# Output projection of two row blocks by seven block products instead of eight, in a hybrid attention layer

## The chip, the cores and the metric

The kernel runs on one core of a Trainium2 chip. A core has a matrix engine (TensorE; "PE" in the profile, and "PEld" for its weight loads), VectorE ("DVE"), ScalarE ("ACT"), GpSimd ("POOL") and SyncE ("SP"), which here only starts DMAs. Each engine works through its own queue in order and waits for the others by semaphores. Weights come from DRAM into SBUF by 16 DMA engines; matmuls write to eight banks of PSUM. The metric is the device time of one execution in microseconds, the median of several runs.

## The reference

One decoder layer for 512 tokens and 1024 channels, in float32. What matters here is the end of its first sub-layer:

```
merged = sigmoid(g_a) * (y_fox @ w_fox_proj) + sigmoid(g_b) * (y_sb @ w_sb_proj)
attn_out = merged @ w_o                                # (512, 1024) @ (1024, 1024)
x = layer_norm(ALPHA * x + (1 + gt1) * attn_out, ln1_g, ln1_b)
```

`y_fox` and `y_sb` are the outputs of two attention branches with eight heads each, `g_a` and `g_b` columns of the input projection, and `gt1` a row of 1024 numbers that comes from a modulation vector. Behind it stands a gated MLP with its own layer norm.

## The kernel before

**Numbers.** Every product of two float32 matrices is made of three matmuls: each operand is split into a high part (rounded, by ScalarE, `hi_of`) and a low part (the rest, by VectorE, `lo_of`), and `mm3` adds high by high, high by low and low by high in PSUM. The down projection of the MLP already forms its row blocks by seven block products instead of eight (`blocks`, `product`, `phase`).

**Weights.** All weight tiles go through one list of items, each a source in DRAM and a procedure (`add_item`). `weights(i)` first issues loads on SyncE's queue up to four items ahead, into `raw` tiles of 128x1024 with five buffers (`LOADS`); a load also waits until the item four places before it has been read (`paced`). Then it calls the procedures of up to two items ahead (`AHEAD`). `split_proc` makes `wh` and `wl`, 128x1024, with three buffers each (`WBUFS`). Items of the modulation (`ada_proc`, VectorE at L241) are held back until the next item has been processed. Only SyncE's queue keeps the program's order; the other engines' queues are ordered by a planner at compile time, which also hands out whichever buffer of a tag comes free.

**Heads and filler.** The 16 heads run one after the other (`stage_a` scores, `stage_b` transposes, `stage_c` values), the stick-breaking branch first. Between the stages `fill` takes matmuls from `stream`, a list of generators in a fixed order: projections of later heads (`proj`), branch projections (`bproj`), gates (`add_gate`: 24 matmuls and a sigmoid). After the last head the rest of `stream` runs: five gates and the eight fox projections. `bproj` for the fox branch, multiplied by its gate (L656) and added to the other branch's (`merge`, L766), gives one of eight 128x512 tiles of `merged`, transposed (channels by tokens), as `mh` and `ml`.

**Output projection.** `wo_proc` takes 128 rows of w_o, multiplies them by `gt[0]` (the row 1 + gt1) on VectorE at L662, and splits both halves of 512 columns into `woh`, `wol`. These small tiles come from one pool, `z`, of 58 (`NZ`). `o_mm(i, ks)` makes row block i (128 tokens) for both column halves: eight channel tiles, three matmuls each, L922 to L924. Row blocks 0 and 1 are taken in two turns, five channel tiles and then three (`CUT`); `o_norm` adds x and normalises; block 2 follows, `o_turn` transposes blocks 0 and 1, then block 3. The up projection begins with tokens 0 to 255 of its first three tiles. Before the change GpSimd multiplies in the stick-breaking heads (L561) and issues small DMAs; `gate_rows` makes `gt[0]` with it long before the last heads.

Of the kernel before, what the change touches and what calls it, by code (L numbers as in the profile page):

```python
# [8 lines left out]
F32 = mybir.dt.float32  # L9
F32R = mybir.dt.float32r  # L10
# [6 lines left out]
P = 128  # L17
# [26 lines left out]
SS = 10  # L44
GTILES = (3, 5, 7, 8, 12, 16, 20, 24)
WARM = 5, 3, 1
CUT = 5
FILL = (15, 18, 18), (11, 11, 11)


# [1 line left out]
def layer_kernel(ctx: ExitStack, tc: tile.TileContext, out, xT, x, c8, wa0, wa1, bcol, w1, wct, wv, bf,  # L52
# [6 lines left out]
    t13 = [tc.dram_tile([P, 1024], F32, name=f"t13_{p}") for p in range(FP)]  # L59
    wgt = [tc.dram_tile([P, 512], F32, name=f"wgt_{q}") for q in range(FP)]  # L60
    t24 = tc.dram_tile([P, 1024], F32, name="t24")
    grow = [tc.dram_tile([1, D], F32, name=f"grow{i}") for i in range(2)]
    st1 = ExitStack()
    stg = ctx.enter_context(tc.tile_pool(name="stg", bufs=1))
# [25 lines left out]
    def hi_of(o, i, scale=1.0):  # L90
        S.activation(o, i, AF.Copy, scale=scale)

    def lo_of(o, i, hi):
        state["read"] = V.tensor_tensor(o, i, fl(hi), ALU.subtract)  # L94
        return state["read"]
# [52 lines left out]
    def z(dt, s, shape=(P, 512)):  # L148
        return zp.tile(list(shape), dt, name=nm(s), tag="z", bufs=NZ)
# [5 lines left out]


    reads, held, pins, convs = [], [], {}, []
    items, depth = [], [LOADS - 1]
    def add_item(src, proc, cols=1024):
        items.append([src, proc, cols, None, None])  # L160
        return len(items) - 1

    def weights(i, ahead=AHEAD):
        while state["load"] < min(len(items), i + depth[0]):
            it = items[state["load"]]
            if it[2] == 512:
                late = state.get("late")
                it[3] = late.tile([P, 512], F32, name=nm("rl"), tag="rl", bufs=4) if late else z(F32, "rs")
            else:
                it[3] = stg.tile([P, 1024], F32, name=nm("raw"), tag="raw", bufs=LOADS)  # L170
            c = 0
            for src in it[0] if isinstance(it[0], list) else [it[0]]:
                w = src.shape[-1]
                d = nc.sync.dma_start(it[3][:, c : c + w], src)
# [10 lines left out]
        while state["proc"] < min(len(items), i + 1 + ahead):  # L185
            process()
        return items[i][4]

    def release():
        while held:  # L190
# [4 lines left out]

    def process():
        it = items[state["proc"]]
        if state["proc"] in pins:
# [12 lines left out]
        reads.append(state["read"])  # L211
        release()
# [302 lines left out]
    def proj(n, after):  # L515
        ps = bank()
        h, l = weights(n)
        for k in range(KT):
            c = slice(k * P, (k + 1) * P)
            mm3(ps, h[:, c], l[:, c], uh[k], ul[k], k == 0, k == KT - 1)  # L520
            yield 3
        after(ps)

    def stage_a(br, h):
# [120 lines left out]
            S.activation(sg[(br, j)], ps, AF.Sigmoid)  # L645
        return f

    def bproj(br, j, n, after):
        ps = bank()
        h, l = weights(n)  # L650
        for q in range(4):
            c = slice(((j % 2) * 4 + q) * P, ((j % 2) * 4 + q + 1) * P)
            mm3(ps, h[:, c], l[:, c], yh[(br, q)], yl[(br, q)], q == 0, q == 3)
            yield 3
        m = sg.pop((br, j))
        V.tensor_tensor(m, ps, m, ALU.mult)  # L656
        after(m)

    woh, wol = [], []

    def wo_proc(r):
        V.tensor_tensor(r, r, gt[0], ALU.mult)  # L662
        h = [z(F32R, "woh") for _ in range(2)]
        l = [z(F32R, "wol") for _ in range(2)]
        for e in range(2):
            c = slice(e * 512, (e + 1) * 512)
            hi_of(h[e], r[:, c])
            lo_of(l[e], r[:, c], h[e])
        woh.append(h)
        wol.append(l)  # L670

    def wdc_proc(r):
        h = [z(F32R, "wdh") for _ in range(2)]
# [28 lines left out]
    marks = {}  # L702
    seq = PAIRS

    def add_proj(n, after):
        stream.append((proj, (add_item(wct[TILES.index(n)], split_proc), after)))
        flush_sum(len(stream))

    def flush_sum(n):
# [2 lines left out]

    wpi = {}

    def add_bproj(br, j, after):
        if j % 2 == 0:
            wpi[br] = add_item(wp[br, j // 2], split_proc)
        stream.append((bproj, (br, j, wpi[br], after)))
# [36 lines left out]
    bj = list(range(KT))  # L755
    for p, nb in (6, 3), (7, 5):
        add_pair(p)
        for _ in range(nb):
            j = bj.pop(0)
            add_bproj(1, j, lambda m, j=j: ma.__setitem__(j, m))  # L760

    mh, ml = [], []

    def merge(j):
        def f(m):
            V.tensor_tensor(m, m, ma[j], ALU.add)  # L766
            a, b = z(F32R, "mh"), z(F32R, "ml")
            hi_of(a, m)
            lo_of(b, m, a)
            mh.append(a)  # L770
            ml.append(b)
        return f

    wos = [0]

    def add_wo():
        if wos[0] < KT:
            add_item(wo[wos[0]], wo_proc)
            wos[0] += 1

    for j in range(3):
        add_gate(0, j)
    marks["y0"] = len(stream)
    flush_sum(1 << 30)
    for j in range(KT):
        add_bproj(0, j, merge(j))
        if j < 5:
            add_wo()
        if j + 3 < KT:
            add_gate(0, j + 3)  # L790
    skip[0] = 0
    add_ada(24 - adas[0])
    while wos[0] < KT:
        add_wo()
    last_wo = len(items) - 1

    cur = {"n": 0, "g": None}

# [108 lines left out]
    x1 = []  # L907
    lnr = []

    o_st = {}  # L910

    def o_mm(i, ks):
        tb = slice(i * P, (i + 1) * P)
        if i not in o_st:
            xn = [z(F32, "xn") for _ in range(2)]
            for e in range(2):
                nc.sync.dma_start(xn[e], x[tb, e * 512 : (e + 1) * 512])
            o_st[i] = xn, [bank(), bank()]
        ps2 = o_st[i][1]
        for e in range(2):  # L920
            for k in ks:
                PE.matmul(ps2[e], mh[k][:, tb], woh[k][e], start=k == 0, stop=False)  # L922
                PE.matmul(ps2[e], mh[k][:, tb], wol[k][e], start=False, stop=False)  # L923
                PE.matmul(ps2[e], ml[k][:, tb], woh[k][e], start=False, stop=k == KT - 1)  # L924

    def o_norm(i):
        xn, ps2 = o_st.pop(i)
        st = cons.tile([P, 2, 6], F32, name=nm("st"), tag="st", bufs=2)
        for e in range(2):
            ps = ps2[e]  # L930
            V.scalar_tensor_tensor(xn[e], xn[e], ALPHA, ps, ALU.mult, ALU.add)
            V.bn_stats(st[:, e, :], xn[e])
        mu, rs = ln_stats(st)
        for e in range(2):
            V.tensor_scalar(xn[e], xn[e], mu, rs, ALU.subtract, ALU.mult)
        x1.append(xn)
# [134 lines left out]
            m = mm3(ps[:, ts], h[:, c], l[:, c], u2h[:, k, ts], u2l[:, k, ts], k == 0, k == KT - 1)  # L1071
        return m

    for ks in (range(CUT), range(CUT, KT)):
        for i in range(2):
            o_mm(i, ks)
            if ks[-1] == KT - 1:
                o_norm(i)
    for i in range(2, NB):
        o_mm(i, range(KT))  # L1080
        o_norm(i)
        for t in ((0, 1), (2,))[i - 2]:
            o_turn(t)
# [252 lines left out]
def _pack(inputs):  # L1336
# [30 lines left out]
    wpj = np.stack([a["w_fox_proj"], a["w_sb_proj"]]).reshape(2, 4, P, 4, 2, P)  # L1367
    r["wp"] = c(wpj.transpose(0, 3, 2, 4, 1, 5).reshape(2, 4, P, D))
    r["wo"] = c(a["w_o"].reshape(KT, P, D))
# [33 lines left out]
```

## Time and profile before

| | |
|---|---|
| median of 3 runs | 735.8 us (735.76 to 736.32) |
| the profiled execution | 736.08 us, its span 734.3 us |
| granted TensorE clock, mean | 0.997 |
| busy: TensorE, VectorE, ScalarE, GpSimd | 724.3, 599.7, 390.1, 84.5 us |
| matmuls | 3442 |
| DMA | 131.96 MB, of which 12.85 MB written |

Times in the profile count from the first instruction. The last stage of the last head ends near 284.4 us, the last fox projection near 333.7 us, the output projection of blocks 0 to 2 near 366.3 us. A line such as "L94 DVE TENSOR_TENSOR wl<-raw,wh 128x1024" names the source line, the engine, the operation, what it writes and reads, and its size; then come its count, its total and mean time, and the idle time of the engine just before it with what ended it. In a timeline row the first number is the start and the second the duration. A stretch row ("284.40:333.65") gives its length and, for each engine, the busy time in it with the count of instructions, then the clock, the share of the DMA engines and GB/s.

### The profile page before, as it was taken

Reading aid. Unit: us, or ns where it says so; the run is one execution under the profiler, and the core shown is the slowest. Engines: PE = TensorE matmul, PEld = TensorE weight load, DVE = VectorE, ACT = ScalarE, POOL = GpSimd, SP = SyncE. Lnnn points to the kernel's source line nnn. Section 1 sums busy time; section 2 is a strip of 40 time slices with the busy share of each in tenths; the row PEclk is TensorE's granted clock in tenths of the full one; section 3 lists DMA queues with packets and bytes.
Section 4 is the critical chain, followed back from the end, with each engine's and each line's share of the span. In section 5 each row is a group of like instructions: output and inputs, shape, how many; then the busy total and the mean of one; then the engine's idle time right before and its main releaser. Section 6 shows DMA issues by size and latency. Waiting matters only on the chain.

```text
span 734.3 us, 9843 instructions
## 1 busy us (share of the span) xinstructions
PE 724.3 (99%) x3442; PEld 604.8 (82%) x3442; DVE 599.7 (82%) x1049; ACT 390.1 (53%) x681; POOL 84.5 (12%) x140
## 2 busy tenths in 40 slices
PE   8999999999999999999999999999999999999995
PEld 5888888888888888888889888888888888888885
DVE  7878799778899896883697999977887878679996
ACT  5576466596885755432065644444453544346550
POOL 1026224343010000000000001000011001000010
PEclk9999999999999999999999999999999999999998
DMA  9944534523332242632075687577799767656734
GB/s 351 404 167 147 196 116 160 185 65 119 135 117 79 95 153 77 206 145 86 1 258 134 218 249 230 177 242 229 206 345 248 212 224 212 214 168 219 228 83 92
DMA packets 45203, 131.96 MB, mean 180 GB/s; under 512 B 6137, under 2 KB 6657, under 8 KB 45153
## 3 DMA queue, kind: packets, MB, share of 16 engines
q1 hardware_dynamic: 37888, 112.61, 44.3%
q0 software_dynamic: 4224, 10.30, 7.4%
q10 hardware_dynamic: 3040, 8.42, 3.1%
q8 instruction: 27, 0.44, 0.2%
q14 instruction: 24, 0.19, 0.1%
HBM read 118.39 MB, written 12.85 MB: 179 GB/s over the span
## 4 chain that ended last, share of the span: by engine, by line
PE 98%; DVE 1%; DMA 0%; issue 0%; DVEq 0%
PE ps L152 19%; PE ps L154 19%; PE ps L153 19%; PE ps L361 6%; PE ps L1131 5%; PE ps L1133 5%; PE ps L1132 5%; PE ps L599 3%; PE ps L581 2%; PE ps L507 2%; PE ps L509 2%; PE ps L508 2%; PE ps L924 2%; PE ps L922 2%; PE ps L923 2%; PE ps L533 1%
## 5 line engine op out<-in xcount | busy, mean ns | idle before, releaser
L217 ACT ACTIVATE wh<-raw 128x1024 fp32r<-128x1024 f32 (+1 forms) x105 | 109.2, 1042 | 107.4 <-PE ps L153 35.2
L94 DVE TENSOR_TENSOR wl<-raw,wh 128x1024 fp32r<-128x1024 f32 (+2 forms) x114 | 137.8, 1210 | 34.2 <-ACT wh L217 33.5
L152 PE MATMUL ps<-u2h,wh 128*128 128x512 f32 (+1 forms) x376 | 141.3, 376 | 0.0
L153 PE MATMUL ps<-u2l,wh 128*128 128x512 f32 (+1 forms) x376 | 141.2, 375 | 0.0
L154 PE MATMUL ps<-u2h,wl 128*128 128x512 f32 (+1 forms) x376 | 141.2, 375 | 0.0
L154 PEld LDWEIGHTS ps<-u2h,wl 128*128 128x128 f32 x376 | 70.8, 188 | 12.9
L152 PEld LDWEIGHTS ps<-u2h,wh 128*128 128x128 f32 x376 | 70.8, 188 | 12.7
L153 PEld LDWEIGHTS ps<-u2l,wh 128*128 128x128 f32 x376 | 70.8, 188 | 12.7
L152 PE MATMUL ps<-uh,wh 128*128 128x512 f32 x200 | 79.5, 398 | 0.0
L154 PE MATMUL ps<-uh,wl 128*128 128x512 f32 x200 | 78.3, 391 | 0.0
L153 PE MATMUL ps<-ul,wh 128*128 128x512 f32 x200 | 77.9, 390 | 0.0
L1184 ACT ACTIVATE cv<-ps,cw 128x512 f32<-128x512 f32 x44 | 34.0, 773 | 46.2 <-PE ps L154 36.2
L1185 DVE SCALAR_TENSOR_TENSOR cv<-ps,cw,cv 128x511 f32<-128x511 f32 x44 | 32.8, 745 | 22.6 <-ACT cv L1184 22.5
L154 PEld LDWEIGHTS ps<-uh,wl 128*128 128x128 f32 x200 | 37.5, 188 | 8.6 <-DVE wl L94 0.3
L153 PEld LDWEIGHTS ps<-ul,wh 128*128 128x128 f32 x200 | 37.6, 188 | 7.5
L152 PEld LDWEIGHTS ps<-uh,wh 128*128 128x128 f32 x200 | 37.5, 188 | 7.3
L241 DVE SCALAR_TENSOR_TENSOR raw<-raw,cbc 128x1024 f32<-128x1024 f32 x32 | 39.6, 1238 | 0.0
L561 POOL TENSOR_TENSOR pt<-pt,om 128x127 f32<-128x127 f32 (+3 forms) x32 | 38.5, 1213 | 1.6 <-DVE om L560 1.5
L181 POOL DMA_DIRECT2D raw<-in_wdp x10 | 8.8, 884 | 245.1 <-DMA raw<-in_wdp 208.4
L1186 DVE SCALAR_TENSOR_TENSOR cv<-ps,cw,cv 128x510 f32<-128x510 f32 x44 | 32.7, 743 | 0.4
L1192 ACT ACTIVATE cv<-cv 128x512 f32<-128x512 f32 x22 | 13.9, 631 | 34.1 <-DVE cv L1186 34.1
L560 DVE TENSOR_TENSOR_SCAN om<-om,dg 128x127 f32<-128x127 f32 (+3 forms) x32 | 27.1, 907 | 2.9 <-ACT om L555 2.9
(238 smaller groups left out, 1552.5 us busy)
## 6 DMA issues: line engine op xcount, KB each, us to landing
raw<-in_wup SPq DMA_DIRECT2D x44, 512.0 KB, 4.7
raw<-in_wa SPq DMA_DIRECT2D x32, 512.0 KB, 3.5
raw<-in_wct SPq DMA_DIRECT2D x25, 512.0 KB, 4.5
raw<-in_wdp SPq DMA_DIRECT2D x20, 512.0 KB, 5.6
wa<-in_wa SPq DMA_DIRECT2D x16, 512.0 KB, 8.6
raw<-in_wdp SPq DMA_DIRECT2D x22, 256.0 KB, 4.5
raw<-t SPq DMA_DIRECT2D x22, 256.0 KB, 4.1
raw<-in_wdp POOLq DMA_DIRECT2D x10, 512.0 KB, 7.4
```

What stands on the lines that cost most here:

```text
L94: state["read"] = V.tensor_tensor(o, i, fl(hi), ALU.subtract)
L152: PE.matmul(ps, wh, ah, start=first, stop=False)
L153: PE.matmul(ps, wh, al, start=False, stop=False)
L154: return PE.matmul(ps, wl, ah, start=False, stop=last)
L217: state["hi"] = S.activation(h[:, 0:cols], r[:, 0:cols], AF.Copy)
L241: state["read"] = V.scalar_tensor_tensor(wt[:, c], wt[:, c], 1.0, cbc[:, c] if by is None else by, ALU.mult, ALU.mult, accum_out=o)
L361: PE.matmul(grp[g], w, u, start=j == 0 and n == 0, stop=j == KT - 1 and n == (1 if g == 7 else 2))
L561: G.tensor_tensor(pt[b][:, s : e - 1], pt[b][:, s : e - 1], om[:, s + 1 : e], ALU.mult)
L1131: PE.matmul(ps, ah, bh, start=first, stop=False, skip_group_check=onto)
L1132: PE.matmul(ps, ah, bl, start=False, stop=False, skip_group_check=onto)
L1133: return PE.matmul(ps, al, bh, start=False, stop=last, skip_group_check=onto)
L1184: S.activation(t, ps, AF.Identity, bias=cw[:, n, 3:4], scale=cw[:, n, 2:3])
```

## The change

Write the first two row blocks and the four pairs of 128-row blocks of scaled w_o as 2x2 blocks. Their product takes seven block products a pair: `wo_five` makes five, on five PSUM banks (`ob`: `pa`, `y`, `z2`, `zz`, `w`) that stay taken from its first call on, and two more are added onto `pa` and `w` after `pa` has been copied and `w` subtracted. The column sums of `merged` that they need are made on VectorE and ScalarE by `wo_sums`, right after the second tile of a pair is merged; so fox projections and gates run in the order `JO` (0, 4, 1, 5, ...).

The sums of the weight blocks are made by GpSimd. w_o is packed in pairs and loaded once as eight raw items during the last heads (`add_scale`: pair 0 behind the projections of the seventh pair of heads, pair 1 behind those of the eighth, pairs 2 and 3 behind the second and third gate). `scale_a` and `scale_b` multiply it by `gt[0]` and store it in DRAM (`swo`), form the sums and store them (`two`). Later `swo` is loaded as items for `wo_proc`, which now only splits, and `two` as items for `split_proc`, used by `wo_five`. A list `live` keeps `weights` from processing ahead while all three `wh` buffers are in use. Block 2's first three channel tiles run before the last `wo_five`.

```diff
+JO = (0, 4, 1, 5, 2, 6, 3, 7)
...
+    def scale_a(p):
+        def f(r):
+            G.tensor_tensor(r, r, gt[0], ALU.mult)
+            G.dma_start(swo[p][:, 0:1024], r)
+            return r
+        return f
+
+    def scale_b(p, k):
+        def f(r):
+            a, lo, hi = items[k][4], slice(0, 512), slice(512, 1024)
+            G.tensor_tensor(r[:, lo], r[:, lo], gt[0][:, hi], ALU.mult)
+            G.tensor_tensor(r[:, hi], r[:, hi], gt[0][:, lo], ALU.mult)
+            G.dma_start(swo[p][:, 1024:2048], r)
+            G.tensor_tensor(a[:, lo], a[:, lo], a[:, hi], ALU.add)
+            G.tensor_tensor(a[:, hi], a[:, hi], r[:, lo], ALU.add)
+            G.dma_start(two[p][:, 1024:2048], a)
+            G.tensor_tensor(r[:, lo], r[:, lo], a[:, lo], ALU.add)
+            G.tensor_tensor(r[:, hi], r[:, hi], r[:, lo], ALU.add)
+            G.dma_start(two[p][:, 0:1024], r)
+        return f
...
-        V.tensor_tensor(r, r, gt[0], ALU.mult)
...
+    def wo_sums(p):
+        a, o = mraw.pop(p), mraw.pop(p + 4)
+        s, h, l = z(F32, "os"), z(F32R, "oh"), z(F32R, "ol")
+        c = [slice(q * P, (q + 1) * P) for q in range(4)]
+        V.tensor_tensor(s[:, c[0]], a[:, b1], a[:, b0], ALU.subtract)
+        V.tensor_tensor(s[:, c[1]], o[:, b0], a[:, b0], ALU.subtract)
+        V.tensor_tensor(s[:, c[2]], s[:, c[1]], a[:, b1], ALU.add)
+        V.tensor_tensor(s[:, c[3]], s[:, c[2]], o[:, b1], ALU.subtract)
...
+        hi_of(h[:, n], s[:, n])
+        lo_of(l[:, n], s[:, n], h[:, n])
+        hi_of(s4[0][:, c[p]], s[:, c[3]])
+        lo_of(s4[1][:, c[p]], s[:, c[3]], s4[0][:, c[p]])
...
+    def wo_five(p, ta, tb):
...
+        h, l = weights(ta, 3)
+        pa, y, z2, zz, w = ob
+        todo = [(y, so[p][2], (h[:, lo], l[:, lo])), (z2, (mh[p + 4][:, b0], ml[p + 4][:, b0]), (h[:, hi], l[:, hi])),
+                (pa, (mh[p][:, b1], ml[p][:, b1]), (woh[p][0], wol[p][0]))]
+        for n in (0, 1, 2) if p < 3 else (0, 2, 1):
+            wo_mm(*todo[n], *ends)
+            yield 3
+        used(ta)
+        h, l = weights(tb, 3)
+        for ps, a, c in ((zz, 0, hi), (w, 1, lo)):
+            wo_mm(ps, so[p][a], (h[:, c], l[:, c]), *ends)
+            yield 3
+        used(tb)
...
-    for ks in (range(CUT), range(CUT, KT)):
-        for i in range(2):
-            o_mm(i, ks)
-            if ks[-1] == KT - 1:
-                o_norm(i)
...
+    S.activation(p1, pa, AF.Copy)
+    V.tensor_tensor(u2, p1, y, ALU.subtract)
+    V.tensor_tensor(u3, u2, zz, ALU.add)
+    V.scalar_tensor_tensor(xa[0], xa[0], ALPHA, z2, ALU.mult, ALU.add)
+    V.scalar_tensor_tensor(xa[1], xa[1], ALPHA, u3, ALU.mult, ALU.subtract)
+    V.tensor_tensor(xa[0], xa[0], u3, ALU.add)
+    V.tensor_tensor(xa[1], xa[1], w, ALU.subtract)
+    o_norm(0, xa)
+    V.scalar_tensor_tensor(xb[1], xb[1], ALPHA, u2, ALU.mult, ALU.subtract)
+    o_mm(2, range(3, 4))
+    for k in range(4):
+        wo_mm(pa, (mh[k + 4][:, b1], ml[k + 4][:, b1]), (woh[k + 4][0], wol[k + 4][0]), False, k == 3, True)
+    for k in range(4):
+        wo_mm(w, so[k][3], (woh[k + 4][1], wol[k + 4][1]), False, k == 3, True)
+    V.scalar_tensor_tensor(xb[0], xb[0], ALPHA, pa, ALU.mult, ALU.add)
+    V.tensor_tensor(xb[1], xb[1], w, ALU.subtract)
+    o_norm(1, xb)
```

The order of the late stream, with b for a fox projection, g for a gate, f for `wo_five` and w for the load and split of a scaled half pair: b0 g3 w b1 g4 f0 b2 w g5 b3 g6 f1 w g7 b4 w b5 w b6 w b7 f2 w, block 2's first three tiles, f3 w.

More of the change, by code (lines that the diff above doesn't have):

```diff
@@ new lines, in wo_mm @@
+    def wo_mm(ps, a, b, first, last, onto=False):
+        PE.matmul(ps, a[0], b[0], start=first, stop=False, skip_group_check=onto)
+        PE.matmul(ps, a[0], b[1], start=False, stop=False, skip_group_check=onto)
+        PE.matmul(ps, a[1], b[0], start=False, stop=last, skip_group_check=onto)
+    def wo_five(p, ta, tb):
+        if p == 0:
+            ob.extend(bank() for _ in range(5))
+        lo, hi, ends = slice(0, 512), slice(512, 1024), (p == 0, p == 3)
+        h, l = weights(ta, 3)
[11 more added lines that the diff above has]
+        used(tb)
@@ new lines, in add_five, with add_wo, first_rows0, rest @@
+    def add_five(p):
+        ta, tb = add_ring(two[p][:, 0:1024]), add_ring(two[p][:, 1024:2048])
+        stream.append((wo_five, (p, ta, tb)))
+    def add_wo(p, n):
+        add_item(swo[p][:, n * 1024 : (n + 1) * 1024], wo_proc(p + 4 * n, ((0, 1), (1, 0))[n]))
+    xab = []
+    def first_rows0():
+        xab.append(o_rows(0))
+        yield 0
+    def rest(i, ks):
+        o_mm(i, ks)
+        yield 0
+    for n in range(3):
+        add_gate(0, JO[n])
+        if n:
+            add_scale(n + 1)
@@ L797, in layer_kernel, with o_mm @@
+    def o_mm(i, ks):
+        tb = slice(i * P, (i + 1) * P)
+        if i not in o_st:
+            o_st[i] = [bank(), bank()]
+        for e in range(2):
+            for k in ks:
+                wo_mm(o_st[i][e], (mh[k][:, tb], ml[k][:, tb]), (woh[k][e], wol[k][e]), k == 0, k == KT - 1)
     cur = {"n": 0, "g": None}
@@ L908, in layer_kernel, with o_norm @@
     lnr = []
[L910 to L915, printed above, removed]
+    def o_norm(i, xn=None):
+        st = cons.tile([P, 2, 6], F32, name=nm("st"), tag="st", bufs=2)
+        if xn is None:
+            ps2, xn = o_st.pop(i), o_rows(i)
             for e in range(2):
-                nc.sync.dma_start(xn[e], x[tb, e * 512 : (e + 1) * 512])
-            o_st[i] = xn, [bank(), bank()]
-        ps2 = o_st[i][1]
+                V.scalar_tensor_tensor(xn[e], xn[e], ALPHA, ps2[e], ALU.mult, ALU.add)
         for e in range(2):
[L921 to L931, printed above, removed]
             V.bn_stats(st[:, e, :], xn[e])
```

143 lines of the change are left out of this document (100 added, 43 removed).

## The prediction

> **What bounds the kernel now.** I read the page's busy line first, then the chain that ended last, then TensorE's own waits, and last the busy time of the stretches that the change touches.
>
> ```profile
> span 734.3 us, 9843 instructions
> PE 724.3 (99%) x3442; PEld 604.8 (82%) x3442; DVE 599.7 (82%) x1049; ACT 390.1 (53%) x681; POOL 84.5 (12%) x140
> PE 98%; DVE 1%; DMA 0%; issue 0%; DVEq 0%
> PE ps L230 <- DVE warm L107: 1.2, 1, 1.2
> PE ps L230 <- DVE wa L241: 0.6, 2, 0.3
> PE ps L361 <- DVE uh L329: 0.3, 1, 0.3
> 284.40:333.65 49.25, 49.25 (x219) 40.33 (x218) 40.49 (x57) 22.28 (x34) 0.00 (x0) 1.00 0.44 153
> 333.65:366.30 32.65, 32.65 (x146) 27.04 (x145) 14.39 (x31) 4.18 (x7) 0.00 (x0) 1.00 0.14 48
> 200.00:284.40 84.40, 84.40 (x440) 72.05 (x439) 72.42 (x157) 54.76 (x114) 2.05 (x4) 1.00 0.29 101
> ```
>
> TensorE is 98% of the chain, and the three rows are all of its waits on others: 2.1 us, at the start. The stretch rows give busy time of TensorE, weight loads, VectorE, ScalarE, GpSimd. From 200 to 366 us, where everything in the diff lies, TensorE is busy without a gap, so a matmul removed there comes off the end, unless a new wait takes its place. 284.4 to 333.65 us is the last gates and fox projections, 333.65 to 366.3 the output projection of row blocks 0, 1 and 2. It has 144 matmuls (two blocks' 96, block 2's 48) and the tail of two before it, so one costs 32.65 / 144 = 0.2267 us. (Rows call a matmul 389 ns; that is its pipelined length.)
>
> **The matmuls.** Before, blocks 0 and 1 take 2 x 2 x 8 x 3 = 96. After, `wo_five` runs five products of three, four times: 60; the two late loops, onto `pa` and `w`, 12 each: 84. Block 2 keeps 48, only moved. Twelve go: 12 x 0.2267 = **2.72 us**. That is the whole gain.
>
> **What VectorE and ScalarE get.** Columns below: line, engine, shape, count, then total and mean ns.
>
> ```profile
> L662 DVE TENSOR_TENSOR raw<-raw,gt 128x1024 f32<-128x1024 f32 x8 | 9.8, 1220 | 1.0 <-DMA raw<-in_wo 0.9
> L94 DVE TENSOR_TENSOR wol<-raw,woh 128x512 fp32r<-128x512 f32 x16 | 10.7, 683 | 0.0
> L94 DVE TENSOR_TENSOR wl<-raw,wh 128x1024 fp32r<-128x1024 f32 x7 | 8.5, 1221 | 2.9 <-ACT wh L217 2.9
> L217 ACT ACTIVATE wh<-raw 128x1024 fp32r<-128x1024 f32 (+1 forms) x105 | 109.2, 1042 | 107.4 <-PE ps L153 35.2
> L550 DVE TENSOR_SCALAR pt<-pt,sm 128x128 f32<-128x128 f32 (+3 forms) x32 | 10.2, 383 | 0.3
> L94 DVE TENSOR_TENSOR ptc<-ps,ptc 128x384 fp32r<-128x384 f32 x16 | 8.7, 546 | 0.0
> L91 ACT ACTIVATE ptc<-ps 128x384 fp32r<-128x384 f32 x16 | 7.9, 493 | 0.1
> 333.53 0.39 PE L154 MATMUL ps<-yh,wl 128*128 128x512 f32 x1
> 333.96 0.69 DVE L656 TENSOR_TENSOR sg<-ps,sg 128x512 f32<-128x512 f32 x1 [0.23 <-PE ps L154]
> 335.17 0.68 DVE L766 TENSOR_TENSOR sg<-sg,sg 128x512 f32<-128x512 f32 x1
> ```
>
> The scaling by `gt` leaves VectorE: 9.8 us less, 7.3 of it after 284.4. Added there: eight splits of the sums, 8 x 1.22 = 9.8 (ScalarE 8 x 1.04 = 8.3); four `wo_sums`, each four 128-column operations (at most 0.38), one low half of 384 (0.55) and one of 128 (0.38), about 2.4 each, 9.8 in all; and two `wol` splits more than the window had, 1.4. So 40.5 - 7.3 + 21 = 54 us in a stretch that grows by 60 + 18 matmuls to 49.25 + 17.7 = 67 us: 81%, against 82% now. ScalarE goes to about 33 of 67. Neither becomes the bound on average. Locally: the last fox matmul starts at 333.53, the merged sum ends at 335.85, 2.3 us later. Four sums (1.5), high (0.5) and low half (0.55) bring the first products' operand at about 4.9 us. `wo_five` 0 to 2 stand behind a gate, 24 matmuls or 5.4 us; number 3 behind 15 + 18, 7.5 us. So they are covered, by half a microsecond where VectorE is free at once, and not if a 1.22 us split is in front; an operand late by that costs 0.7 us at one place. I take 0.3 us in all, with 0 and 3 (four places) as bounds.
>
> **The end.** The copy of `pa` must be done before the late loop adds onto `pa`, and `xa[1] - w` before the loop onto `w`; TensorE's queue holds the rest of block 2 behind both. `pa` closes nine matmuls before `wo_five` ends; one ScalarE copy then has that 2.0 us and 6 more matmuls (1.4). After the copy VectorE has six operations of 0.69, ending about 2.5 us after `w` closes, where 18 matmuls (4.1 us) stand. `o_norm(1)` follows the last of the 24: two operations, two statistics and a chain that takes 5 us, beside 24 matmuls, 5.4 us. Covered, thinly; zero, at most 1 us. The transposes and the first up weights then move with the rest.
>
> **GpSimd, DRAM and SyncE's queue.** GpSimd gets 28 operations and 16 stores of 512 KB; SyncE's queue gets 24 loads for w_o where it had 8, and the first eight now stand ahead of weights that TensorE needs sooner. That is 8.4 MB stored and 8.4 MB more loaded over some 150 us, 112 GB/s beside the 101 and 153 of the stretch rows at shares of 0.29 and 0.44: the DMA engines are not filled. Block 0's `x` loads move ahead of `wo_five` 3's; the tiles that they take came free with the last projection's inputs, so they hold up nothing.
>
> ```profile
> L561 POOL TENSOR_TENSOR pt<-pt,om 128x511 f32<-128x511 f32 x8 | 10.6, 1330 | 0.0
> 124.01 1.08 POOL L561 TENSOR_TENSOR pt<-pt,om 128x511 f32<-128x511 f32 x1
> gt<-grow POOLq DMA_DIRECT2D x1, 512.0 KB, 4.0
> wgt<-wg POOLq DMA_DIRECT2D x1, 256.0 KB, 2.3
> out<-xn POOLq DMA_DIRECT2D x4, 256.0 KB, 5.3
> raw<-in_wp SPq DMA_DIRECT2D x8, 512.0 KB, 3.8
> raw<-in_wct SPq DMA_DIRECT2D x25, 512.0 KB, 4.5
> L637 POOL DMA_DIRECT2D gt<-grow x3 | 1.7, 578 | 14.4 <-DMA grow<-growt 14.4
> 260.85 0.33 SPq L174 DMA_DIRECT2D raw<-in_wa  x1
> 275.32 0.39 PE L152 MATMUL ps<-uh,wh 128*128 128x512 f32 x1
> 284.43 0.45 PE L152 MATMUL ps<-yh,wh 128*128 128x512 f32 x1
> 121.17 2.35 DVE L94 TENSOR_TENSOR wl<-raw,wh 128x1024 fp32r<-128x1024 f32 x1
> 121.46 0.87 POOL L561 TENSOR_TENSOR pt<-pt,om 128x383 f32<-128x383 f32 x1
> ```
>
> A 512-column operation takes 1.08 us alone, 1.33 on average; one of 1024 isn't in the trace, 2.2 to 2.7. One group is 2.4 + 6 x 1.2 + 4 issues of 0.58 = 12 us, and it has a wait inside: `r` may be rewritten only when its store to `swo` has read it. A 512 KB store from GpSimd I take at 4.0 us (nearest in size, though a load), bounds 2.3 and 5.3. GpSimd has nothing else then (2.05 us busy from 200 to 284.4), so its own time is free; what waits for it is the raw buffers. Five of them serve all loads, and two stay taken for the length of a group.
>
> Groups 0 and 1 come a head or more before what follows. Group 2: its second half is loaded behind the row at 260.85 (a load that waits for the same modulation sum), lands at 264.7; two operations and an issue, 267.7; two more and the store, first buffer free at 274.7; `r` waits until 271.7, second buffer free at 278.7. The third gate's weights slide behind it to 261.2, land at 265.7, are split by 268.5; TensorE needs them at 275.3: covered by 7 us. The first fox weights then need a buffer. The pool hands out whichever is free, and the gate's buffer (268.5) and the modulation's (about 270) come free before GpSimd's: loaded by 271, split by 278, needed at 284.43. The next gate and the fifth follow with 5 us to spare. So GpSimd is hidden, and I take zero, if the buffers are given so.
>
> VectorE and GpSimd collide: beside the GpSimd row at 121.46 a `wl` of 1.22 took 2.35. In 200 to 284.4 us VectorE has 21 such operations from two SBUF tiles; GpSimd would be busy a third of it. If half collide and lose 0.4 to 1.1, VectorE loses 4 to 12 us less the 2.4 it is spared, where 84.4 - 72.4 = 12 are idle; its work is a head (some 10 us) ahead of TensorE. I take zero; bounds 0 and 3.
>
> The Trainium skill (GPSIMD Engine Reference, Key points) says that GpSimd shares its SBUF interfaces with VectorE and contends with instructions of two SBUF inputs: it speaks against moving this work to GpSimd, and the 2.35 us agree. By it the collisions are the 3 us of that bound; by the idle 12 us they are hidden.
>
> **Sum.** -2.72 + 0.3 = -2.4 us. On the profiled execution's 736.08 (span 734.3 and 1.8 around it) that is 733.7; it lies 0.3 above the median of the runs, 735.8, from which I forecast **733.4 us**, own range 732.7 to 734.3.
>
> **Rivals.** *Small waits take it back.* The thin covers above and the collisions come together: 1.3 to 4.2 us lost, 734.4 to 737.3, say 735.5. For it: VectorE above 80% and operands half a microsecond early. Against: TensorE has no wait there at the same load today.
>
> *The raw buffers turn in order, and GpSimd's group 3 holds the loads (slower).* Then the first fox weights wait for group 2's second buffer (278.7, split by 285, no loss), but the fifth gate's wait for group 3's. With stores of 4.3 us: second half loaded at 275.5, landed 279.3, stored from 282.4 and so rewritten from 286.7, free at 294. The gate lands at 298.5, is split by 300.9; its third matmul was due 48 + 2 matmuls after 284.43, at 295.8. A wait of 5.1, and 0.3 at the next load: 735.8 - 2.7 + 5.4 = **738.5**. It decides from a wait of 4.2 us on; with stores of 2.3 the wait is 1 (734.1), with 5.3 8 (741). For it: the two buffers are in truth held. Against: other banks and buffers in this kernel are held while the rest turn.
>
> By the Trainium skill (TensorE: Matmul & The Clock Gate, Part 1) an idle window of about 3.4 us halves the clock for as long again; an estimate of 1.7 us more by that page, which no row here shows.
>
> *Not doing what it says*: the count of matmuls follows from the loops, so I give this nothing.
>
> **Chances.** Forecast 0.58, and 0.03 for below 732.7; small waits 0.22, of which 0.03 beyond 4.2 us; held buffers 0.17, a third of it within 0.2%. A measurement of this kernel tells about 0.2% (1.5 us) from no change. Faster 0.58 + 0.03 = 0.61; same 0.19 + 0.06 = 0.25; slower 0.03 + 0.11 = 0.14. The range 732.7 to 737.4 leaves out 0.03 below and 0.14 above.
>
> **What would show it.** Right: 3430 matmuls, no wait of TensorE between 200 and 370 us beyond a few tenths, transposes 2.4 us earlier. Small waits: rows of TensorE on `os` halves or `wl` below 1 us each. Held buffers: SyncE's queue waiting on stores to `two`, and one TensorE wait of microseconds at a gate near 295 us. Wrong altogether: VectorE's low halves late before 284 us, or the late loops waiting on `xa`.

## The result and the profile after

The change makes the kernel slower: 761.6 us (median of four runs, 759.28 to 762.24) against 736.1 us for the kernel before beside it (735.76 to 737.64), a ratio of 1.0335 with a 95% interval of 1.0318 to 1.0352. Forecast were 733.4 us and a range that ended at 737.4; even the slowest rival, 738.5, lies 23 us below. The profiled execution took 759.28 us.

The page of the kernel after: span, busy line and the engines' shares of the chain that ended last.

```profile
span 757.5 us, 9996 instructions
PE 731.2 (97%) x3430; PEld 604.2 (80%) x3430; DVE 625.2 (83%) x1078; ACT 400.9 (53%) x698; POOL 136.9 (18%) x184
PE 75%; DVE 11%; DMA 7%; ACT 4%; issue 2%; POOL 1%; SPq 0%; DVEq 0%; ACTq 0%; POOLq 0%
```

The twelve matmuls are gone (3442 to 3430). But TensorE, which was 98% of the chain, is 75% of it now: VectorE, DMA and ScalarE have become what it waits for. Two stretches of it, TensorE's main waits, and two of SyncE's (engine, line, what it waited for: total us, times, longest):

```profile
190.00:284.00 94.00, 90.00 (x462) 75.26 (x461) 86.53 (x164) 57.12 (x123) 40.09 (x37) 1.00 0.46 171
284.00:320.00 36.00, 27.65 (x104) 20.44 (x102) 20.59 (x28) 13.38 (x21) 14.89 (x14) 0.86 0.71 249
PE ps L154 <- ACT wh L229: 5.1, 2, 4.2
PE ps L154 <- ACT yh L93: 3.0, 1, 3.0
PE ps L1072 <- DVE xn L1062: 2.4, 2, 2.0
PE ps L594 <- DVE s L472: 2.2, 1, 2.2
SPq L176 <- DVE m L96: 22.3, 1, 22.3
SPq L176 <- DMA two<-raw: 10.1, 3, 4.8
```

TensorE is idle for 4 us in the last heads, where GpSimd works, and for 8.4 us between 284 and 320, where the gates and first products stand; there the granted clock is 0.86 as well. The waits are on halves of weights and of operands, as the forecast feared, but not by tenths.

VectorE in the last heads and gates, 190 to 304 us, grouped by line (count, total us, mean ns): first the kernel after, then an experiment with the same loads and stores and no arithmetic on GpSimd (`x5_nogp` below).

```profile
L563 DVE TENSOR_SCALAR pt<-pt,sm 128x128 f32<-128x128 f32 (+3 forms) x28 | 19.1, 743 | 0.2
L96 DVE TENSOR_TENSOR wl<-raw,wh 128x1024 fp32r<-128x1024 f32 x12 | 18.7, 1564 | 9.2 <-ACT wh L229 9.2
L253 DVE SCALAR_TENSOR_TENSOR raw<-raw,cbc 128x1024 f32<-128x1024 f32 x7 | 9.8, 1401 | 0.5 <-DMA raw<-in_wa 0.5
L96 DVE TENSOR_TENSOR yl<-yf,yh 128x512 fp32r<-128x512 f32 x5 | 6.3, 1269 | 2.1 <-ACT yh L93 2.1
L96 DVE TENSOR_TENSOR ptc<-ps,ptc 128x384 fp32r<-128x384 f32 x8 | 4.4, 544 | 0.0
```

```profile
L563 DVE TENSOR_SCALAR pt<-pt,sm 128x128 f32<-128x128 f32 (+3 forms) x28 | 8.9, 383 | 0.2
L96 DVE TENSOR_TENSOR wl<-raw,wh 128x1024 fp32r<-128x1024 f32 x14 | 17.0, 1223 | 6.4 <-ACT wh L229 6.4
L253 DVE SCALAR_TENSOR_TENSOR raw<-raw,cbc 128x1024 f32<-128x1024 f32 x9 | 11.0, 1219 | 1.3 <-DMA raw<-in_wa 1.3
L96 DVE TENSOR_TENSOR yl<-yf,yh 128x512 fp32r<-128x512 f32 x5 | 3.5, 693 | 2.1 <-ACT yh L93 2.1
L96 DVE TENSOR_TENSOR ptc<-ps,ptc 128x384 fp32r<-128x384 f32 x8 | 4.4, 548 | 0.0
```

Four groups are longer: 28 x 0.36 + 12 x 0.34 + 7 x 0.18 + 5 x 0.58 = 18.4 us. Those that read PSUM (the last row of each) are not. The longest group of victims, the scaling of `pt` by `sm`, has a single tile as input and was not in the forecast's count of 21.

### The profile page after: what moved, and what is told of

It is laid out like the page before. It is cut to its first block, busy times and chain, and to the rows that moved or that the text cites. A ratio compares the mean times of both kernels' runs of the same rounds, so it can differ in the third digit from the quotient of the medians.

```text
span 757.5 us, 9996 instructions
## 1 busy us (share of the span) xinstructions
PE 731.2 (97%) x3430; PEld 604.2 (80%) x3430; DVE 625.2 (83%) x1078; ACT 400.9 (53%) x698; POOL 136.9 (18%) x184
## 4 chain that ended last, share of the span: by engine, by line
PE 75%; DVE 11%; DMA 7%; ACT 4%; issue 2%; POOL 1%; SPq 0%; DVEq 0%; ACTq 0%; POOLq 0%
PE ps L154 14%; PE ps L155 14%; PE ps L156 14%; PE ps L373 6%; PE ps L1275 5%; PE ps L1276 5%; PE ps L1277 5%; DVE wl L96 2%; DMA raw<-two 2%; DMA raw<-in_wct 2%; PE ps L519 2%; PE ps L521 2%; PE ps L520 2%; ACT wh L229 1%; ACT pt L558 1%
## 5 line engine op out<-in xcount | busy, mean ns | idle before, releaser
L96 DVE TENSOR_TENSOR wl<-raw,wh 128x1024 fp32r<-128x1024 f32 (+2 forms) x122 | 150.7, 1236 | 47.3 <-ACT wh L229 46.4
L229 ACT ACTIVATE wh<-raw 128x1024 fp32r<-128x1024 f32 (+1 forms) x113 | 117.5, 1042 | 124.7 <-PE ps L155 47.7
L154 PE MATMUL ps<-yh,wh 128*128 128x512 f32 x64 | 26.4, 413 | 7.2 <-ACT wh L229 4.2
```

What stands on the lines that cost most here:

```text
L154: PE.matmul(ps, wh, ah, start=first, stop=False)
L229: state["hi"] = S.activation(h[:, 0:cols], r[:, 0:cols], AF.Copy)
```

## The experiments

Each kernel ran beside the kernel before on one chip (medians of that 735.7 to 736.3 us). Times of one run are told as such.

### Is it the order of the loads?

A load waits (`paced`) for the reading of the item four places before it; the point that is noted for a raw item of w_o is whatever low half was issued last, which explains the 22.3 us on `m` above. `x1_anchor` notes the last real reading of an item instead (`still` marks the raw items of w_o):

```diff
+        if getattr(it[1], "still", False):
+            state["read"] = next(r for r in reversed(reads) if r is not None)
         reads.append(state["read"])
```

> The whole change, but a raw item of w_o no longer takes the last low half traced as the point that the load four places later waits for: it takes the read of the item before it. Theory A (these points lie too late: in the changed kernel SyncE's queue waits 22.3 us for m, 11.1 for ptc and 10.5 for yl, none of which reads a load's buffer): the three waits go, TensorE's waits between 190 and 330 us fall from some 13 us to under 4, the clock stays at 1.0, and the time is 735 to 742 us. Theory B (GpSimd holds two of five raw buffers): the waits move to stores to two, and the time stays above 750.

Measured: 763.4 us, ratio 1.0379 [1.0359, 1.0398]. The wait on `m` was gone, and SyncE waited for the stores instead:

```profile
SPq L176 <- DMA two<-raw: 38.1, 7, 8.9
```

The theory of the stale points fell; the waits moved to the stores, as theory B had it.

### Taking parts away

`x2_loads` keeps the eight raw loads and drops the stores and GpSimd's arithmetic, `x5_nogp` keeps loads and stores and drops the arithmetic, `x3_late` drops all of it; `wo_five` and `wo_proc` then take w_o as it is, where nothing was stored.

```diff
     def scale_a(p):
         def f(r):
-            G.tensor_tensor(r, r, gt[0], ALU.mult)
-            G.dma_start(swo[p][:, 0:1024], r)
             return r
...
     def add_scale(p):
-        add_item(wo[p][:, 0:1024], scale_a(p))
-        add_item(wo[p][:, 1024:2048], scale_b(p, len(items) - 1))
+        return
```

> The eight raw items of w_o are only loaded: no GpSimd operation, no store; the later loads read w_o itself, so neither the scaling by gt nor the weight sums are in the output. Points of waiting as in the change. Theory A: SyncE's queue still waits for m, ptc and yl, and the time is above 750 us. Theory B: the buffers come free at once and the time is 734 to 740.

> The raw items of w_o are left out altogether (the scaling by gt and the weight sums are not in the output); the late stage with its 84 matmuls is that of the change. Theories A and B: no wait before 284 us, twelve matmuls less, and only the waits of the late stage that the changed kernel shows (xn at the transposes 2.4, oh 0.9): 734 to 737 us. Theory C (the late stage itself, VectorE and ScalarE, makes the loss): above 742.

> The change without GpSimd's 28 operations, but with its 16 stores and all loads (neither the scaling nor the sums are in the output). Theory A: the points of waiting are as late as before, above 750 us. Theory B, or VectorE losing to GpSimd at the SBUF: buffers are held for some 5 us instead of 12 and nothing collides, under 745.

Measured: 744.8 us (one run), 744.5 us (ratio 1.0122 [1.0103, 1.0140]) and 744.8 us (one run). `x2_loads` lies between its two theories, `x3_late` is where theory C put it. So the loss has two parts. The new late stage by itself costs 8.6 us where it was to spare 2.7, that is 11.3 us; loads and stores add nothing to that; GpSimd's 28 operations add 16.7.

### GpSimd: buffers held, or VectorE held off?

The 28 operations also keep raw buffers for longer. `y1_hold` holds them without arithmetic, by two more stores a group to one spare place, which follow one another; `y2_port` computes on a scratch tile and holds nothing more.

```diff
             G.dma_start(two[p][:, 1024:2048], a)
+            G.dma_start(spare[p], a)
+            G.dma_start(spare[p], r)
             G.dma_start(two[p][:, 0:1024], r)
```

> The kernel without GpSimd arithmetic (loads and 16 stores, 744.8 us), and in each of its four groups two more stores to a spare DRAM tile, both to the same place, so that they and the last store of the group follow one another and the raw buffers are held some 8 us longer, as the six sums held them; GpSimd still computes nothing. It leaves out the scaling and the sums. Theory H (the 16.7 us between the full change and this base come from raw buffers held for the length of a group): 753 to 762 us, with waits of SyncE's queue on the stores of 8 us and more a group. Theory P (they come from GpSimd's operations slowing VectorE's): 744 to 747 us, and the 128-column TENSOR_SCALAR on pt stays at 383 ns.

> The kernel without GpSimd arithmetic again, and GpSimd gets 28 operations of the sizes of the change (four of 1024 and 24 of 512 columns) at the same places, but on a scratch tile that nothing else reads, behind the stores, so that they hold no raw buffer. The scaling and the sums are left out of the result. Theory P: 755 to 762 us, TENSOR_SCALAR pt<-pt,sm near 740 ns between 190 and 304 us, against 383. Theory H: 744 to 746 us, whatever the TENSOR_SCALARs take, as VectorE's work would be ahead of TensorE.

`y1_hold`: 744.3 us (one run), TENSOR_SCALAR unchanged. SyncE waits 17.4 us for the spare stores there, and 16.6 us for stores to `two` in `x5_nogp`, more than the 10.1 us in the change itself, and neither run loses the 16.7 us:

```profile
SPq L176 <- DMA two<-raw: 16.6, 3, 8.9
```

So holding buffers isn't enough for the 16.7 us. But it has a part in the change. There the third group starts late and works at GpSimd's pace: its first instruction starts at 263.2 us and its last, a store to `two`, at 286.43 (in `y1_hold` 255.6 and 266.2). The gate's load waits 4.8 us for a store to `two` and goes out at 292.51; in `x5_nogp` the same load goes out at 277.07. ScalarE splits it at 298.03 and only then copies the values of the last head, and TensorE waits for that head's output (`yh`). Just before, it waits 4.2 us for the first fox weights:

```profile
286.43 0.57 POOL L693 DMA_DIRECT2D two<-raw  x1 [0.30 <-POOL raw L692]
292.51 0.33 SPq L176 DMA_DIRECT2D raw<-in_wct  x1
298.03 1.06 ACT L229 ACTIVATE wh<-raw 128x1024 fp32r<-128x1024 f32 x1 [3.34 <-DMA raw<-in_wct]
294.74 0.80 PE L154 MATMUL ps<-yh,wh 128*128 128x512 f32 x1 [4.16 <-ACT wh L229]
303.13 0.50 PE L154 MATMUL ps<-yh,wh 128*128 128x512 f32 x1 [3.04 <-ACT yh L93]
```

```profile
277.07 0.33 SPq L176 DMA_DIRECT2D raw<-in_wct  x1
```

All of SyncE's waits for stores in the change lie behind 284 us. The last head's softmax starts 9.2 us later than in `x5_nogp` (272.72 against 263.56), the split of its output 15.8 us later (302.45 against 286.67). So some 9 of the 16.7 us arise before any load waits for a store, and the rest in the gates, where late heads, held buffers and the lower clock come together. No run separates these.

`y2_port` gave 762.9 us (one run), the number that the rival theory had forecast, and for another reason: its scratch operations depended on nothing and were placed at 51 to 118 us, ahead of the products that GpSimd owes the stick-breaking heads. TensorE waited 7.7 us for those. It tells nothing of the last heads. `y3_port` ties each pair of scratch operations behind a store of its group:

```diff
+    def busy(d, n):
+        with tc.issue_after(d.ins):
+            for m in range(2):
+                c = slice(0, 1024) if n == 1 else slice(m * 512, (m + 1) * 512)
+                if m < n:
+                    G.tensor_tensor(scr[:, c], scr[:, c], cbc[:, c], ALU.mult)
```

> The run before this one that was to make GpSimd collide without holding buffers didn't: the order gave its 28 operations to the time from 51 to 118 us, ahead of GpSimd's own work for the first heads. Here each pair of them is tied behind a store of its group, so that they run between 190 and 305 us as in the change; they work on a scratch tile, hold no raw buffer, and the scaling and the sums are left out. Theory P (operations of VectorE lengthened by GpSimd's): 755 to 762 us, TENSOR_SCALAR pt<-pt,sm at 650 to 750 ns in the mean and wl near 1.55 us between 190 and 304 us. If holding and colliding are needed together: about 745 us with the long TENSOR_SCALARs, as the holding alone gave 744.3.

Measured: 774.1 us (one run), 29 above the same kernel without the scratch operations, and above what either theory forecast. TensorE's largest waits, then the timeline, GpSimd first (start, duration, what), then VectorE, then the summary of the scalings of `pt` (shortest, median and longest in ns):

```profile
PE ps L156 <- DVE wl L96: 10.3, 3, 6.2
PE ps L548 <- DVE m L96: 6.4, 1, 6.4
```

```profile
236.86 2.42 POOL L682 TENSOR_TENSOR scr<-scr,cbc 128x1024 f32<-128x1024 f32 x1
...
241.81 5.05 POOL L682 TENSOR_TENSOR scr<-scr,cbc 128x512 f32<-128x512 f32 x4
246.80 0.58 POOL L695 DMA_DIRECT2D two<-raw  x1
247.40 2.51 POOL L682 TENSOR_TENSOR scr<-scr,cbc 128x512 f32<-128x512 f32 x2
```

```profile
237.08 2.75 DVE L96 TENSOR_TENSOR yl<-yf,yh 128x512 fp32r<-128x512 f32 x1
...
242.71 8.28 DVE L565 TENSOR_SCALAR pt<-pt,sm 128x128 f32<-128x128 f32 x4
250.91 1.14 DVE L96 TENSOR_TENSOR pl<-ps,ph 128x512 fp32r<-128x512 f32 x2
```

```profile
L565 DVE TENSOR_SCALAR pt<-pt,sm x32: 286/416/7294, 183.6 to 283.5; 128x128 f32<-128x128 f32 x8, 128x384 f32<-128x384 f32 x8, 128x256 f32<-128x256 f32 x8, 128x512 f32<-128x512 f32 x8
```

`yl`, 0.69 us alone, starts just behind a GpSimd operation and ends half a microsecond after that has ended (239.28). The first scaling of 242.71 takes 7.3 us: it comes through when GpSimd's six operations in a row are over (249.91). GpSimd's operations keep their 1.26 us. The next work of that head (`pl`) starts at 250.91, and TensorE waits for it:

```profile
251.64 0.50 PE L547 MATMUL ps<-m,s 128*128 128x512 f32 x1 [2.83 <-DVE pl L96]
```

The stores still hold raw buffers here, some of them behind scratch operations, but SyncE waits 9.0 us for stores to `two`, less than in `x5_nogp` (16.6). So VectorE being shut out is enough for a loss of this size. It is a harder case than the change: the trains of GpSimd operations are closer, and a `wl` (1.22 us alone) took 7.8 us beside one.

The Trainium skill (SBUF — State Buffer, Who interferes with whom) says that VectorE and GpSimd share one pair of ports by an exclusive lock, and that a `tensor_scalar` in a two-port mode needs it as an operation of two SBUF inputs does; and VectorE: DVE Perf Modes (Mode 2×_2P) says that a float32 `tensor_scalar` enters such a mode. The rows agree (in `x5_nogp` a scaling of 512 columns takes 481 ns, a `yl` of that width 693), and these pages name the 28 operations that the forecast left out.

### The late stage: late loads, or a bad order?

`z1_depth` is `x3_late` with the pacing lifted from the last head on: `weights` paces a load only while `depth[0]` is below `LOADS`. Each load then goes out as soon as a buffer is free. The same line lets loads go five items ahead, not four, so the two are not told apart. `z3_both` adds an order by hand: the splits of the sums' weights behind the sums, and at the end block 0's normalising ahead of the rest.

```diff
         if n == 15:
             lim[0] = len(stream)
+            depth[0] = LOADS
```

```diff
+    def split_after(r):
+        with tc.issue_after(state["sa"].ins), tc.issue_after(state["sv"].ins):
+            return split_proc(r)
...
-    o_norm(0, xa)
-    V.scalar_tensor_tensor(xb[1], xb[1], ALPHA, u2, ALU.mult, ALU.subtract)
+    n0 = o_norm(0, xa)
+    with tc.issue_after(n0.ins):
+        V.scalar_tensor_tensor(xb[1], xb[1], ALPHA, u2, ALU.mult, ALU.subtract)
```

> The late stage alone (w_o's loads in its own tiles, no GpSimd group, 744.5 us; scaling and weight sums left out), with loads from the last head on no longer held back to a point in VectorE's order: each goes out as soon as a raw buffer is free. Theory L1 (the 11 us of the late stage come from loads that go out late): 737 us or less, the first wait at wo_five 0 (1.89 us) and the wait for the high half of a load gone. Theory L2 (the order of VectorE's and ScalarE's queues): 742 to 745. Theory I (too much work on VectorE for the stretch, whatever the order): 743 to 746.

> The late stage alone with the early loads and, besides, an order by hand: the splits of each sum item stand behind the sums of the same block on ScalarE and VectorE, and at the end VectorE's normalising of block 0 stands ahead of the work for blocks 1 and 2. Scaling and weight sums are left out. Theories L1 and L2 together: 733 to 737 us, no wait of TensorE over 0.8 us between 285 and 380, clock 1.00 between 360 and 380. L1 alone: as the run with early loads, within 1 us. Theory I: 742 to 746, with VectorE above 90% busy between 300 and 360 and the same waits at other places.

Measured: 734.3 us (one run) and 743.6 us (ratio 1.0097 [1.0079, 1.0116]). Late loads it is; the theories of the order and of too much work fell. The rows of `x3_late` that show it (a load on SyncE's queue; ScalarE, which stands behind it; TensorE), then the load's twin in `z1_depth`:

```profile
293.52 0.80 SPq L176 DMA_DIRECT2D raw<-in_wo  x2
297.83 1.06 ACT L229 ACTIVATE wh<-raw 128x1024 fp32r<-128x1024 f32 x1 [4.13 <-DMA raw<-in_wo]
298.79 0.61 ACT L93 ACTIVATE mh<-sg 128x512 fp32r<-128x512 f32 x1
PE ps L828 <- ACT oh L93: 1.9, 1, 1.9
```

```profile
277.19 8.21 SPq L178 DMA_DIRECT2D raw<-in_wo  x2
364.33 1.91 PE L1063 MATMUL ps<-ident,xn 128*128 128x128 f32 x16
```

The load that the first sums need goes out at 293.5, since the reading that it waits for stands late on VectorE (SyncE waits 15.6 us). ScalarE idles 4.1 us on it with the next merged tile queued behind (`mh`), so the sums are late, and TensorE waits 1.9 us on a sum (`oh`) that could have been formed earlier. With the loads 16 us earlier these waits are gone, and the transposes of blocks 0 and 1 begin at 364.33; before, at 366.40:

```profile
366.40 1.91 PE L945 MATMUL ps<-ident,xn 128*128 128x128 f32 x16
```

The order by hand made a new wait, 4.2 us before the transposes of block 1, whose normalising it had put back.

`f3_again` repeats `z1_depth` for an interval.

> The bare late stage with unpaced loads once more, for an interval (one run gave 734.27). It leaves out the scaling and the sums. If the 12 matmuls less come through: 734.0 to 734.6 us, a ratio of 0.998, at most 1.000. If that run was a lucky one: 735.5 or more.

Measured: 734.8 us, ratio 0.9987 [0.9977, 0.9996] of 735.9. The gain is there, some 1.0 us of the 2.7, in a kernel that leaves out the weight sums.

### Putting it together again

With the pacing lifted: `d1_full` is the whole change, `e1_dram` all but GpSimd's arithmetic, `f1_loads` all but stores and arithmetic, and `f2_spread` is `e1_dram` with one group at each of the last four pairs of heads (the edits are those above; `f2_spread` moves `add_scale`).

> The whole change with only the loads from the last head on no longer paced. The late stage gained 10.3 us by this (744.5 to 734.3). If the two losses add up: 761.6 - 10.3 = 751 us, 748 to 753. If they hide one another, or the raw buffers bind once the pacing is gone: 756 us or more.

> Everything of the change but GpSimd's 28 operations, with the unpaced loads: the seven products, the eight first loads, the 16 stores to DRAM and the loads from there. It leaves out the scaling and the sums. If the round trip through DRAM is free once loads go out early: 734.0 to 735.5 us, like the bare late stage (734.3, one run), which would make GpSimd's operations the whole of the other 18 us. If 16.8 MB more traffic and buffers held for the stores cost something that the pacing hid until now: 737 us or more.

> The bare late stage with unpaced loads (734.3 us) and the eight first loads of w_o into raw buffers, but no stores and no arithmetic: a buffer is free again when its load has landed. Scaling and sums are left out. The run with the 16 stores took 746.3 us, with one wait of 8.6 us behind a load that had no buffer. Theory B (stores hold the buffers): 734 to 736 us, no such wait. Theory Q (eight loads more in SyncE's queue are enough to delay the ones behind): 741 us or more.

> The eight loads and 16 stores with the groups one each at the last four pairs of heads, none beside the gates, unpaced loads, no arithmetic (scaling and sums left out). If only the groups beside the gates do harm (the last one holds two buffers when the next gate's load is due): 734 to 736 us. If a group's held buffers do harm wherever they stand: 740 to 748 us, as in the spread run with VectorE's sums (747.8), with a wait for the value weights near 150 us.

| | us | ratio |
|---|---|---|
| `d1_full` | 753.2 | 1.0245 [1.0206, 1.0285] |
| `e1_dram` | 746.3 | 1.0143 [1.0121, 1.0166] |
| `f1_loads` | 735.8 | 1.0004 [0.9991, 1.0017] |
| `f2_spread` | 743.6 | one run |

`d1_full` is 8.4 us faster than the change, not the 10.3 that the late stage gained; its four runs reach from 752.0 to 759.0. In `e1_dram` the round trip through DRAM is not free once nothing else delays the loads. With the stores it costs 10.5 us more than without, and the eight loads themselves about 1.0. In `e1_dram` SyncE waits for a buffer that a store to `two` still reads; the row of that wait, the gate's load behind it, ScalarE and TensorE:

```profile
SPq L178 <- DMA two<-raw: 17.6, 4, 8.7
286.94 0.55 SPq L178 DMA_DIRECT2D raw<-in_wct  x1
293.80 1.06 ACT L231 ACTIVATE wh<-raw 128x1024 fp32r<-128x1024 f32 x1 [8.14 <-DMA raw<-in_wct]
294.76 0.61 ACT L93 ACTIVATE yh<-yf 128x512 fp32r<-128x512 f32 x1
295.43 0.80 PE L154 MATMUL ps<-yh,wh 128*128 128x512 f32 x1 [8.59 <-ACT yh L93]
296.02 0.63 PE L156 MATMUL ps<-uh,wl 128*128 128x512 f32 x1
296.45 0.63 PE L154 MATMUL ps<-uh,wh 128*128 128x512 f32 x1
```

The output of the last head (`yh`), ready to be split at 286.4, stands on ScalarE behind the split of a gate that TensorE needs later, and that gate's weights are late. After the 8.6 us matmuls start every 0.43 us, and from 299.3 on every 0.23; the granted clock is 0.50 from 295.4 to 299.0, 3.6 us. `f2_spread` shows that groups do harm in the heads too; its longest wait, 2.8 us on a `wh`, ends at 218 us.

So late pacing (`x3_late`, 744.5) and held buffers (`e1_dram`, 746.3) are two ways to the same late loads, and do not add: with both, `x5_nogp` took 744.8.

### Another engine for the arithmetic

`v1_vec` is `d1_full` with `V` for `G` in `scale_a` and `scale_b`; `v2_spread` puts its groups at the last four pairs of heads. `e2_gp_act` is `d1_full`, `e3_vec_act` is `v1_vec`, each with `pt` scaled by ScalarE:

```diff
-                V.tensor_scalar_mul(pt[b][:, c], pt[b][:, c], sm[:, 8 + i : 9 + i])
+                S.activation(pt[b][:, c], pt[b][:, c], AF.Copy, scale=sm[:, 8 + i : 9 + i])
```

> The whole change with unpaced loads, and the scaling and the weight sums made by VectorE in place of GpSimd, at the same places: 4 x (1.22 + 6 x 0.69) = 21 us more on VectorE, about what the collisions took from it (18 us by the rows), and no collisions. Theory P: the time of the run with GpSimd less a little, 746 to 751 us, with VectorE near 98% busy from 200 to 290 us. If what counts is not VectorE's time but GpSimd's slow chain: 735 to 738 us.

> The same with the four groups spread over the last four pairs of heads, one each, from about 140 us on, where the stretches of 20 us have 2 to 4 us of VectorE idle. Theory P: what VectorE is given fits into its idle time, 734 to 738 us, and at 734 no faster than the bare late stage (734.3). If the stores that a sum waits for stop VectorE's queue: 738 to 745 us, with waits of VectorE on stores to swo of 2 us and more.

> The whole change with unpaced loads (753.2 us), and the 32 scalings of pt by sm, VectorE's TENSOR_SCALARs, made by ScalarE instead (some 11 us more on ScalarE, 60 of 94 us busy between 190 and 284). If these operations are the main victims of GpSimd (8.0 of 13.9 us lost by the rows of that run): 740 to 746 us. If whichever operation of VectorE stands next (wl, yl) is held off for as long in their place: 748 to 754 us, with wl and yl longer than 1.43 and 1.22 us.

> The scaling and the sums on VectorE, no arithmetic on GpSimd, unpaced loads (749.2 us), and pt scaled by ScalarE, so that VectorE has 10.7 us less between 190 and 304. If VectorE's time is what binds there: 736 to 741 us. If it is the order of its queue and the buffers held while the sums stand between other work: 745 us or more, with VectorE below 90% busy.

Measured: 749.2 (one run), 747.8 (ratio 1.0162 [1.0145, 1.0179]), 760.2 and 758.4 us (one run each). VectorE does the 21 us of arithmetic itself for 2.9 us over `e1_dram`; given to GpSimd it costs 6.9. Taking the scalings off VectorE helped neither kernel. `v2_spread` and `e2_gp_act` lie above the ranges of both their theories, and what sets their times is open. In `e2_gp_act` the next operation of two tiles takes the scalings' place, 1.81 us where it was 1.27 in `d1_full`, and ScalarE waits 3.0 us for VectorE's reciprocal with other heads' work queued behind:

```profile
L255 DVE SCALAR_TENSOR_TENSOR raw<-raw,cbc 128x1024 f32<-128x1024 f32 x8 | 14.4, 1812 | 1.7 <-DMA raw<-in_wa 1.6
```

No version with the whole computation came below the kernel before. The bare late stage, with no scaling and no sums, is 0.13% faster at best, so there is little left to win this way.

## Why the prediction was wrong

**The matmuls**: right in count, and -2.72 us is about what the transposes gained in `z1_depth` (2.1 us). Of it 1.0 us reached the end in `f3_again`.

**"I take 0.3 us in all, with 0 and 3 (four places) as bounds"**: 11.3 us measured (`x3_late`). The step priced operations on engines that take them when their input is there. It held in `z1_depth` (TensorE's waits on `oh` were 0.4 us), where the weights come early. What it left out is when the late stage's loads go out, which hangs on readings that stand late on VectorE, and that ScalarE's queue holds merged tiles behind a split that waits for a load.

**"GpSimd is hidden, and I take zero, if the buffers are given so"**: loads and stores add nothing without GpSimd's arithmetic (`x5_nogp` as `x3_late`), but only because the pacing had made the same loads late. Without pacing it is 10.5 us. The rival of held buffers had the mechanism, and its marks (SyncE waiting for stores to `two`, one wait of microseconds near 295 us) are the rows of `e1_dram`, and of the change too (10.1 us of waiting for stores, 4.2 us ending at 294.74); its price of 5.4 us was too small since it saw the gate late, and not the last head's output behind the gate's split on ScalarE.

**"VectorE has 21 such operations from two SBUF tiles ... I take zero; bounds 0 and 3"**: 16.7 us in the change as it is, 6.9 with the loads early. This is the largest error. The count left out the 28 scalings of `pt`, more than half of the 18.4 us that VectorE lost, and set the loss against 12 us of idle time. In its window, 200 to 284.4 us, the loss is 14 us by the same sum, more than that. But the sum isn't what decides: VectorE is idle for 7.4 us in that window of the change and TensorE waits all the same. Nor was it a cover that VectorE is a head ahead of TensorE: the scalings stand in a head's own chain, and in `y3_port` one of them that was held came through as a wait of TensorE within a microsecond. The 16.7 us also hold what GpSimd's slow third group costs by the buffer that the gate's load waits for; its share is open.

**Clock**: the 1.7 us that the forecast took from the Trainium skill (TensorE: Matmul & The Clock Gate, Part 1) for an idle window is borne out by `e1_dram`: about 3.6 us at half the pace, some eight matmuls at 0.2 us more. In the change it follows the wait of 4.2 us on `wh` and goes on behind the next, of 3.0 us: some sixteen matmuls, about 3 us.

**The sum**: -2.7 + 11.3 (late loads) + 0 (stores and held buffers, hidden by these) + 16.7 (GpSimd's operations) = 25.3 us, against 25.5 measured. This closes by itself, since each part is a difference of two runs taken in this order; in another order the shares differ, as above. What was not tried: raw buffers of their own for w_o, and a spread of GpSimd's operations with gaps.

## What to carry to other kernels

Before work is given to GpSimd, list what VectorE does in the same stretch by ports, not by inputs: float32 `tensor_scalar` from SBUF counts like an operation of two tiles, work from PSUM doesn't. Where VectorE has no idle time, it may be cheaper to let it do the work. An operation that waits for a late load delays everything queued behind it on its engine, so check for each load of a new order when it can go out and which ready work stands behind its first reader.

## What the runs showed of the hardware

VectorE could be held off over several operations of GpSimd, not only over the one that ran: in `y3_port` one scaling of 128 columns, 0.29 us alone, took 7.3 us, over the rest of a train of six GpSimd operations and a DMA issue. But it isn't always so. In the change GpSimd's operations at 232.92, 234.18 and 235.43 follow one another without a gap too, and the scalings that begin beside them took 1.44, 1.46 and 1.88 us, so each got in after an operation or so of 1.28 us; the longest of all 32 took 2.6 us. What decides how long VectorE is held, these runs don't show.

```profile
234.11 5.03 DVE L563 TENSOR_SCALAR pt<-pt,sm 128x128 f32<-128x128 f32 x4
234.18 1.29 POOL L686 TENSOR_TENSOR raw<-raw,gt 128x512 f32<-128x512 f32 x1
235.43 1.28 POOL L688 TENSOR_TENSOR raw<-raw 128x512 f32<-128x512 f32 x1
```
